# Thirty-two bytes of padding in one tile: moving the right side of SBUF onto multiples of 64 bytes

## The chip, the core and the metric

The kernel runs on one core of a Trainium2 chip. The metric is the device time of one launch in microseconds. A profiled execution of the same program gives its span (from the first to the last instruction) and, for every instruction, the time it took.

## What is computed

One layer of a hybrid backbone over 1024 latent tokens and 256 context tokens with 1024 channels. After an RMS norm with a modulation, one projection of 10272 columns feeds two branches. Branch A is a bidirectional gated delta rule in chunks with a short convolution on q, k and v; branch B is a differential softmax attention of 8 heads with a rotary position code. Each branch is normed, gated with SiLU and projected; the two are merged by sigmoid gates, projected once more and added to the input.

```python
h = rms_norm(x) * (1.0 + scale[:, None]) + shift[:, None]
qkv_a, z_a, a_raw, b_raw, q_b, k_b, v_b, z_b, gates = split_cols(h @ w_in)
o_a, o_ac = gdn_bidirectional(gdn_prepare(...ctx...), gdn_prepare(...latent...), update_ctx)
...
p = jax.nn.softmax(s, axis=-1)
attn = p[:, :, 0] - lam * p[:, :, 1]
return jnp.einsum('bhqk,bkhv->bqhv', attn.astype(v.dtype), v)
...
merged = g_a * (y_a.reshape(b, length, GDN_WIDTH) @ w_oa) + g_b * (y_b.reshape(b, length, DIFF_V_WIDTH) @ w_ob)
return merged @ w_out
```

## The kernel before

**Rounded products.** Nearly all large products are made of three: an operand x is split into a rounded part (type float32r, "xh") and the rest ("xl"), and x·y is taken as xh·yh + xh·yl + xl·yh, added up in PSUM. These are the *rounded products* of the title. Small products of the delta rule and all transposes stay plain float32.

**Streams.** The kernel is written as generators that hand out one instruction at a time with an estimated duration and the tokens it waits for; a planner (`flow`, `turn_flow`) picks the next one by its own model of the engines and so fixes the order on each engine. The estimates are constants in the code; no address enters them.

**Stages in order of time.**

- To about 420 us: loading, the norm, the first projections with the convolution (`mm<-hs,wh`, `mm<-wh,hs`).
- About 420 to 740 us: the projections q, k, v of the attention (`part_flow`, 256 columns wide), beside the preparation of the delta rule (`gdn_prep`).
- About 740 to 1340 us: the gate projections (`fill_flow`, 512 columns wide), beside the scan of the delta rule (`scan`, `out_chunk`).
- About 1340 to 1767 us: the attention and, in between, the merge of branch A. `scores` (L1536) makes `s<-kk,qh` and `s<-kk,ql`: per block of 128 queries and each of the two maps, pieces of 512, 512 and 256 columns. `turns` transposes the weights of the softmax (`t<-ct,S`). `att_out` (L1647) makes `v<-ah,vh`, `v<-al,vh`, `v<-ah,vl`, 256 columns wide, ten key blocks of three products for a pair of query blocks. `merge_` (L1791) makes `ma<-y,wh` and `ma<-y,wl`, 512 wide, 24 products for one bank.
- 1767 to 1856 us: `b_main` (L1909) projects branch B: `mb<-yh,wh`, `mb<-yl,wh`, `mb<-yh,wl`, 512 wide, 384 products.
- To the end: `o_main` (L2097) makes the last projection in seven products of half-size blocks (`x<-...`, `z<-...`, 512 wide).

In a name such as `mb<-yh,wh` the first operand is the one that is streamed through the array and the second is the weights that are loaded ahead of it.

**Where tiles lie.** SBUF is used from two sides. Pools of `side="left"` are stacked upwards from the constants, pools of `side="right"` downwards from a fixed top (`spool`, L711). On the right, from the delta rule on (`gdn_first`, L1047), there stand from the top down: g2 with the tags X, kq and qk (X lowest, qk at the top), g3 and g1, g4 (the scan), later a2 and a0 (the attention: qh, ql, kk, vh, vl and the scores S), and at the end yq (yh, yl), bp and rp. Tags of g2 are used again under other names: X and kq hold kk and qh of every second head, and weights at the end. On the left stand hs and the weights wh, wl of the projections, later a1 (ah, al), yp2 (y), ws2 (wh, wl of the merge and of `b_main`) and lp (half of the operands of `o_main`; the other half is in bp and rp).

The operands' first bytes, as the program places them, modulo 64:

| product | streamed operand | weights |
|---|---|---|
| mm (all projections) | left, 0 | left, 0 |
| s | kk: right, 32 | qh, ql: right, 32 |
| v | ah, al: left, 0 | vh, vl: right, 32 |
| ma | y: left, 0 | wh, wl: left, 0 |
| mb | yh, yl: right, 32 | wh, wl: left, 0 |
| x, z | bh, bl: by turns left, 0, and right, 32 | ah, al: on the same side as bh |

For example kq begins at byte 215008 of each partition, X at 204768, qk at 224224, yq at 121120; ws2 begins at 22528.

Of the kernel before, what the change touches and what calls it, by code (L numbers as in the profile page):

```python
# [17 lines left out]
P = 128  # L18
D = 1024
KT = D // P  # L20
L = 1024
LC = 256
LT = L + LC
# [20 lines left out]
class Block:  # L44
# [1040 lines left out]
    def gdn_prep(self, h):  # L1085
# [6 lines left out]

        def keys():
            S = lambda nm, shape: self.gh[0].tile(shape, F32, tag=nm, name=nm)
            kq, qk = S("kq", [P, LT + L]), S("qk", [P, 2, 2, 2, P])
            kT, qT = kq[:, :LT], kq[:, LT:]
            tk = yield DMA, 3.3, self.kT_t, lambda: nc.sync.dma_start(kq, self.gkq[h])
            tk = tq = self.later(tk, 1.5)
            return kT, qT, qk, tk, tq
        mine = None  # L1100
        if self.gram == h:
            mine = yield from keys()

        te = [None] * 2
        for d in range(2):
# [3 lines left out]
            te[d] = yield ACT, 1.18, [t], lambda: nc.scalar.activation(X[:, d], X[:, d], AF.Exp, scale=-1.0), AF.Exp  # L1109
        yield lambda: self.gram == h  # L1110
        kT, qT, qk, tk, tq = mine or (yield from keys())

        tX, tQ = [[], []], []
# [1097 lines left out]
```

## Time and profile before

| | us |
|---|---|
| median of 3 runs | 1938.72 |
| lowest and highest | 1936.44, 1939.59 |
| the profiled execution's own time | 1938.76 |
| its span | 1936.6 |
| chain from the first mb product to the end of the last x product | 166.0 |

How it is read: the page sums each engine's busy time and follows one chain of waits back from the last instruction. A matmul's recorded duration is longer than the distance to the next one, because the products overlap in the array; the view of one tile lists the least, median and longest duration of a group, and the chain gives start, length and count of a row of products, so that length by count is the distance from start to start. The granted TensorE clock was 1.0 in every stretch of this execution.

### The profile page before, as it was taken

Reading aid. Unit: us, or ns where it says so; the run is one execution under the profiler, and the core shown is the slowest. Engines: PE = TensorE matmul, PEld = TensorE weight load, DVE = VectorE, ACT = ScalarE, POOL = GpSimd, SP = SyncE. Lnnn points to the kernel's source line nnn. Section 1 sums busy time; section 2 is a strip of 40 time slices with the busy share of each in tenths; the row PEclk is TensorE's granted clock in tenths of the full one; section 3 lists DMA queues with packets and bytes.
Section 4 is the critical chain, followed back from the end, with each engine's and each line's share of the span. In section 5 each row is a group of like instructions: output and inputs, shape, how many; then the busy total and the mean of one; then the engine's idle time right before and its main releaser. Section 6 shows DMA issues by size and latency. Waiting matters only on the chain.

```text
span 1936.6 us, 37454 instructions
## 1 busy us (share of the span) xinstructions
PE 1899.9 (98%) x13807; PEld 1673.9 (86%) x13807; DVE 1450.8 (75%) x3613; ACT 1064.0 (55%) x2189; POOL 679.4 (35%) x610
## 2 busy tenths in 40 slices
PE   6999999999999999999999999999999999999999
PEld 4888888899999998888888888888988888888887
DVE  4687998957887887767865865338996979985577
ACT  4543444426233563677576655448885868883222
POOL 3200000005441342343433232326766657671203
PEclk9999999999999999999999999999999999999999
DMA  9144545575545567667785565666336474226542
GB/s 334 56 139 96 138 95 136 125 190 175 168 144 177 183 191 226 226 198 228 213 291 179 192 196 158 214 232 229 127 124 201 165 240 147 83 88 223 184 147 87
DMA packets 383038, 336.39 MB, mean 174 GB/s; under 512 B 142609, under 2 KB 323443, under 8 KB 381831
## 3 DMA queue, kind: packets, MB, share of 16 engines
q1 hardware_dynamic: 382855, 333.99, 55.0%
q8 instruction: 109, 1.79, 0.4%
q14 instruction: 74, 0.61, 0.1%
HBM read 222.14 MB, written 111.79 MB: 172 GB/s over the span
## 4 chain that ended last, share of the span: by engine, by line
PE 84%; DVE 6%; DMA 4%; ACT 3%; issue 2%; POOL 1%; SPq 1%; DVEq 0%; ACTq 0%; POOLq 0%
PE mm L56 42%; PE s L56 7%; PE v L56 5%; PE chain L56 5%; PE mb L56 5%; PE ma L56 4%; PE x L56 3%; PE t L63 3%; PE out L56 3%; PE gram L56 1%; DVE S L1567 1%; DVE ac L595 1%; DMA sk<-gkq 1%; PE pz L56 1%; PE tr L63 1%
## 5 line engine op out<-in xcount | busy, mean ns | idle before, releaser
L56 PE MATMUL mm<-hs,wh 128*128 128x512 f32 (+1 forms) x2048 | 648.3, 390 | 1.5 <-DVE hs L408 1.4
L56 PEld LDWEIGHTS mm<-hs,wh 128*128 128x128 f32 x2048 | 371.1, 189 | 58.6 <-DVE hs L408 2.0
L56 PE MATMUL mm<-hs,wl 128*128 128x512 f32 (+1 forms) x1024 | 397.4, 388 | 1.0 <-POOL wl L886 1.0
L56 PE MATMUL mm<-wh,hs 128*128 128x256 f32 (+1 forms) x1792 | 332.8, 286 | 0.2 <-ACT sq L978 0.2
L56 PEld LDWEIGHTS mm<-wh,hs 128*128 128x128 f32 x1792 | 280.8, 191 | 0.8 <-ACT sq L978 0.5
L1567 DVE TENSOR_SCALAR_CACHE_REDUCE S<-s,rsq 128x512 f32<-128x512 f32 (+1 forms) x384 | 239.5, 654 | 27.6 <-PE s L56 24.9
L56 PE MATMUL mm<-wl,hs 128*128 128x256 f32 (+1 forms) x896 | 255.6, 285 | 0.0
L1604 POOL TENSOR_TENSOR S<-S 128x1280 f32<-128x1280 f32 x64 | 188.9, 2955 | 92.2 <-ACT S L1597 90.9
L56 PEld LDWEIGHTS mm<-hs,wl 128*128 128x128 f32 x1024 | 193.8, 189 | 29.8 <-POOL wl L886 1.4
L1580 ACT ACTIVATE S<-S,mn 128x1280 f32<-128x1280 f32 x128 | 175.2, 1371 | 51.8 <-DVE mn L1579 51.4
L56 PEld LDWEIGHTS mm<-wl,hs 128*128 128x128 f32 x896 | 171.3, 191 | 0.1
L595 DVE SCALAR_TENSOR_TENSOR ac<-xc,convT,ac 128x1284 f32<-128x1284 f32 (+1 forms) x96 | 138.7, 1448 | 11.4 <-ACT ac L593 10.8
L56 PE MATMUL s<-kk,qh 128*128 128x512 f32 (+1 forms) x384 | 142.7, 372 | 1.9 <-DVE S L1567 1.6
L56 PE MATMUL s<-kk,ql 128*128 128x512 f32 (+1 forms) x384 | 133.2, 359 | 0.2 <-DMA ql<-qd 0.2
L1641 DVE TENSOR_TENSOR al<-t,ah 128x512 fp32r<-128x512 f32 (+1 forms) x192 | 106.8, 594 | 7.6 <-ACT ah L1636 6.3
L580 POOL MEMSET xc<- 128x2 f32 (+1 forms) x64 | 3.6, 101 | 298.2 <-ACT sq L629 113.7
L1160 DVE TENSOR_TENSOR ts<-ts,tmp 80x31 f32<-80x31 f32 (+15 forms) x248 | 94.3, 380 | 6.0
L56 PE MATMUL ma<-y,wh 128*128 128x512 f32 x256 | 93.0, 409 | 1.7 <-DVE g L1814 1.7
L1158 DVE TENSOR_TENSOR tmp<-ab,ts 80x31 f32<-80x31 f32 (+15 forms) x248 | 89.2, 360 | 6.8 <-DMA ab<-da 1.4
L1323 ACT ACTIVATE vd<-chain,edk 128x128 f32<-128x128 f32 x144 | 52.3, 370 | 76.1 <-PE chain L56 70.6
L1636 ACT CAST ah<-t 128x512 fp32r<-128x512 f32 (+1 forms) x192 | 88.0, 521 | 8.9 <-PE t L63 8.2
L56 PE MATMUL v<-al,vh 128*128 128x256 f32 x320 | 90.5, 283 | 0.7 <-DVE al L1641 0.6
(296 smaller groups left out, 4312.6 us busy)
## 6 DMA issues: line engine op xcount, KB each, us to landing
wr<-in_w_in_dram SPq DMA_DIRECT2D x48, 512.0 KB, 5.8
hx<-in_w_in_dram SPq DMA_DIRECT2D x64, 256.0 KB, 4.4
x<-xq SPq DMA_DIRECT2D x64, 256.0 KB, 5.2
X<-gcd SPq DMA_DIRECT2D x8, 1280.0 KB, 8.3
kd<-col SPq DMA_DIRECT2D x40, 256.0 KB, 2.2
xq<-X SPq DMA_DIRECT2D x16, 640.0 KB, 8.8
kk<-kd SPq DMA_DIRECT2D x16, 640.0 KB, 6.1
kq<-gkq SPq DMA_DIRECT2D x8, 1152.0 KB
```

The source lines that it names most:

```text
L56: self.nc.tensor.matmul(out, lhsT, rhs, start=start, stop=stop)
L63: self.nc.tensor.transpose(out, src, self.ident[:src.shape[0], :src.shape[0]])
L580: x["e"].append((yield PL1, 0.1, [old], lambda: nc.gpsimd.memset(xc[:, a:b], 0.0)))
L595: t = yield DV2, 1.21e-3 * wd, [t], lambda: nc.vector.scalar_tensor_tensor(ac[:, :wd], xc[:, j:j + wd], self.convw(j, x["ct"]), ac[:, :wd] ...
L1158: t = yield DV2, n * w / 960.0 + 0.08, [t if j else self.later(t, 2.5), t1], lambda: V.tensor_tensor(tv, ab[:, j + 1:, j:j + 1].to_broadca ...
L1160: t = yield DV2, n * w / 960.0 + 0.08, [t, t1], lambda: V.tensor_tensor(ts[:, j + 1:, :w], ts[:, j + 1:, :w], tv, ALU.subtract)
L1323: td = yield ACT, 0.251, [t], lambda: nc.scalar.activation(vd, pc[:, 1], AF.Copy, scale=self.edk[:, c, g:g + 1])
L1567: e = yield DVE, 0.675 if m == 512 else 0.408, [e, self.sfree[c].get(n - 4 + c)], lambda: self.nc.vector.tensor_scalar(x["S"][c][:, o:o + ...
L1580: x["x"].append((yield ACT, 1.36, [e], lambda: nc.scalar.activation(S, S, AF.Exp, bias=x["mn"][:, c:c + 1], scale=-1.0, accum_out=w["l0"][ ...
L1604: e = yield POOL, 2.9, [e], lambda: self.nc.gpsimd.tensor_tensor(S0, S0, S1, ALU.add)
L1636: e = yield ACT, 0.48 if nb == 4 else 0.27, [t, y["old", k]], lambda: self.nc.scalar.copy(y["ah", k][:, :, q], pv)
L1641: t = yield DVE, 0.603 if k < 2 else 0.322, [e, y["old", k]], lambda: self.nc.vector.tensor_tensor(y["al", k][:, :, q], pv, y["ah", k][:, ...
```

## The change

The tile kq of `keys` (in `gdn_prep`) is allocated with eight more float32 values per partition and used without them. It is the first time that kq is allocated, so the slot of the tag in pool g2 grows from 9216 to 9248 bytes.

```diff
         def keys():
             S = lambda nm, shape: self.gh[0].tile(shape, F32, tag=nm, name=nm)
-            kq, qk = S("kq", [P, LT + L]), S("qk", [P, 2, 2, 2, P])
+            kq, qk = S("kq", [P, LT + L + 8])[:, :LT + L], S("qk", [P, 2, 2, 2, P])
             kT, qT = kq[:, :LT], kq[:, LT:]
             tk = yield DMA, 3.3, self.kT_t, lambda: nc.sync.dma_start(kq, self.gkq[h])
```

The top of the right side and qk stay where they are; kq, X and all pools opened below g2 begin 32 bytes lower, at addresses that are multiples of 64 (kq at 214976, X at 204736, yq at 121088). The left side and the right side of the earlier stages (to the end of the convolution) are not moved.

## The prediction

> **What bounds the kernel now.** I read the page first, for which engine is full; then the waits of TensorE, for what is left to gain by supplying it better; then the chain of waits at the end, where the time of one product can be read off.
>
> ```profile
> span 1936.6 us, 37454 instructions
> PE 1899.9 (98%) x13807; PEld 1673.9 (86%) x13807; DVE 1450.8 (75%) x3613; ACT 1064.0 (55%) x2189; POOL 679.4 (35%) x610
> PE 84%; DVE 6%; DMA 4%; ACT 3%; issue 2%; POOL 1%; SPq 1%; DVEq 0%; ACTq 0%; POOLq 0%
> ```
>
> TensorE is busy for 1899.9 of 1936.6 us and is 84% of the chain.
>
> ```profile
> PE mp L56 <- DMA wa<-in_w_ada_dram: 10.6, 1, 10.6
> PE tp L63 <- ACT sil L330: 5.3, 1, 5.3
> PE ma L56 <- DVE g L1814: 1.7, 2, 0.9
> ```
>
> Of its waits the two that count, 10.6 and 5.3 us, are at the very start, before the shifted memory is in use; the next is 1.7 us in all. So behind the front no supplier is late, and the change can act in one way only: through the time that a product itself takes. A product's recorded duration overlaps its neighbours', so I take its time as the distance from start to start, which the chain gives as a piece's length by its count:
>
> ```profile
> 1761.01 5.73 PE ma L56 x24
> 1766.74 89.60 PE mb L56 x384
> 1856.34 21.84 PE x L56 x96
> 1878.18 10.91 PE z L56 x48
> 1889.09 43.66 PE x L56 x192
> ```
>
> From 1766.74 on the chain is TensorE alone, with no idle time. All of these are rounded products of one shape, 128x128 by 128x512. Yet mb takes 89.60/384 = 233.3 ns, and x and z together 76.41/336 = 227.4 ns. The views of the single tiles say the same in durations (least, median, longest):
>
> ```profile
> L56 PE MATMUL mb<-yh,wh x128: 393/396/399, 1766.6 to 1855.5; 128*128 128x512 f32 x128
> L56 PE MATMUL x<-bh,ah x96: 389/389/402, 1856.2 to 1931.9; 128*128 128x512 f32 x96
> L56 PE MATMUL ma<-y,wh x256: 387/395/500, 1350.4 to 1766.1; 128*128 128x512 f32 x128
> L56 PE MATMUL mm<-wh,hs x1516: 277/283/387, 419.7 to 735.6; 128*128 128x256 f32 x190
> L56 PE MATMUL v<-al,vh x320: 276/280/386, 1331.8 to 1755.0; 128*128 128x256 f32 x160
> ```
>
> Not one mb product of 128 is under 393 ns, while the x have their median at 389. What differs is where the operands lie. mb streams yh and yl from the right side, which begin 32 bytes past a multiple of 64, against weights on the left, which begin on a multiple. In x and z both operands lie on the same side: both 32 past, or both on a multiple, at the same 389. So, as these rows have it, it isn't the 32 bytes that cost 6 ns, but that the two operands stand at **different** offsets. The timeline of TensorE shows how the quick pace comes about (columns: start, duration, form, count):
>
> ```profile
> 1856.18 0.40 PE L56 MATMUL x<-bh,ah 128*128 128x512 f32 x1
> ...
> 1858.03 0.39 PE L56 MATMUL x<-bh,al 128*128 128x512 f32 x1
> ...
> 1877.56 0.39 PE L56 MATMUL x<-bl,ah 128*128 128x512 f32 x1
> ```
>
> The first eight products after mb take 1.85/8 = 231.3 ns, the next 86 take 19.53/86 = 227.1 ns. With equal offsets the stream needs some eight products to fall into step; with unequal ones it never does, in 384.
>
> **The change part by part.** It adds 32 bytes to the slot of kq. The right side is stacked downwards from a fixed top, so X in the same pool, and every pool opened below (g1, g3, g4, a0, a2, yq, bp, rp), begins 32 bytes lower, on a multiple of 64; qk, above kq, stays, and no rounded product reads it. No instruction, wait, transfer or queue entry is added or moved, and the planner that orders the streams knows no addresses. What is left is the offsets: mb goes from 32/0 to 0/0, v (left al, ah against right vh, vl) from 0/32 to 0/0; s, x and z keep equal ones; the projections mm and the merge ma lie on the left and don't change.
>
> *mb.* 384 products go from 233.3 to 227.1 ns: 384 x 6.2 = **-2.4 us**. They lie alone on the path:
>
> ```profile
> 1767.00:1856.30 89.30, 89.30 (x384) 71.72 (x384) 48.14 (x58) 18.47 (x27) 18.05 (x10) 1.00 0.58 191
> 1856.30:1936.60 80.30, 76.44 (x337) 62.76 (x335) 65.69 (x72) 22.18 (x24) 18.92 (x12) 1.00 0.31 107
> ```
>
> (Stretch and its length, then busy time of PE, weight loads, DVE, ACT and POOL, granted clock, DMA share, GB/s.) The suppliers of mb are busy for 48.1 of 89.3 us at most, so they can follow a pace 3% quicker; if they couldn't, the gain would be 0. Behind it x starts at once, and its later operands have 10.9 us of x products before them.
>
> *x and z.* They fall out of step at each change of side (mb to x, then between x on the left, x on the right and z); at eight products by 4.2 ns, 34 ns each, four or five such changes are **-0.15 us**, at least 0.
>
> *Attention (1340 to 1767).* Here v, s, ma and the transposes t take turns. The chain gives what 256 columns cost in step and out of it:
>
> ```profile
> 503.19 6.70 PE mm L56 x56
> 509.89 0.44 PE tr L63 x4
> 510.33 4.18 PE mm L56 x35
> 514.51 0.44 PE gram L56 x4
> ```
>
> ```profile
> 1742.65 1.42 PE v L56 x12
> ...
> 1744.29 2.13 PE v L56 x18
> ```
>
> mm, at equal offsets, takes 6.70/56 = 119.6 ns; v, at unequal ones, 2.13/18 = 118.3 ns. At this width being in step is the **slower** pace, by 1.3 ns. So the change costs something in v:
>
> ```profile
> L56 PE MATMUL v<-ah,vh 128*128 128x256 f32 x320 | 90.2, 282 | 0.0
> L56 PE MATMUL s<-kk,qh 128*128 128x256 f32 x128 | 36.6, 286 | 0.3 <-DVE S L1567 0.2
> L56 PE MATMUL s<-kk,qh 128*128 128x512 f32 x256 | 106.2, 415 | 1.6 <-DVE S L1567 1.4
> L56 PE MATMUL ma<-y,wl 128*128 128x512 f32 x128 | 52.3, 409 | 0.0
> ```
>
> v has 3 x 320 products and s 2 x 128 of 256 columns, 1216 in all: +1.6 us if all fall into step. Against them stand 512 of s and 384 of ma with 512 columns: ma's median is 395 where x has 389, because a v, an s or a transpose soon interrupts it; up to 896 x 6 = -5.4 us if none did any more. Between these ends I take what the runs allow: after the change v, s and ma no longer disturb each other, transposes and the small sums still do. v comes in runs of 12 and 18, s and ma in twos to fives: three quarters of the 256-wide (+1.2 us) and a third of the 512-wide at 5 ns (-1.5 us), **-0.3 us**.
>
> *Plain (unrounded) products and transposes.* gram, both operands 32 past, takes 0.44/4 = 110 ns, and tr, both on a multiple, the same 110: **0**.
>
> *The other engines and the DMAs.* They meet the same shift, and rows for both sides stand beside each other:
>
> ```profile
> L1881 DVE TENSOR_TENSOR yl<-yl,yh 128x1024 fp32r<-128x1024 f32 x7 | 8.4, 1215 | 1.7 <-ACT yh L1880 1.7
> L317 DVE TENSOR_TENSOR wl<-wr,wh 128x1024 fp32r<-128x1024 f32 x4 | 4.8, 1215 | 0.0
> ```
>
> ```profile
> g<-gt SPq DMA_DIRECT2D x32, 256.0 KB, 4.1
> x<-in_x_dram SPq DMA_DIRECT2D x16, 256.0 KB, 4.1
> ```
>
> Right (yl, and x of the last stage) and left (wl, g): 1215 ns both, 4.1 us both. **0**.
>
> The sum is -2.4 - 0.15 - 0.3 = -2.85 us. The profiled execution took 1938.76 us (its span 1936.6 and 2.2 around it), as good as the median of the runs, 1938.72: **1936.0 us** after rounding.
>
> **The rivals.** *Addresses don't matter*, and mb is slow for a reason of its own; or the shift doesn't arrive where it should. Then the time is 1938.7. For it: mb and x also differ in what runs beside them, and two groups of products are all that the rows compare. Against it: the pace breaks between one product and the next where ma ends and mb begins, and DVE is busier beside x (65.7 of 80.3 us) than beside mb. The Trainium skill speaks for this rival: its page TensorE: Matmul & The Clock Gate, section Step-by-step: what each phase is for, gives TensorE two independent read ports, so that "Loading the next tile's weights doesn't steal SBUF read bandwidth from the running matmul". By that rule the offset of the one against the other could cost nothing and the sum would be 0; the 393 against 389 ns of these rows don't agree with it, as long as nothing else sets mb apart.
>
> *Step is kept all through attention*, interruptions or not: -2.55 for the end, and two thirds to all of 5.4 us instead of a third, with little of the 1.2 us: 1938.7 - 2.55 - 4.2 = 1932.0. For it: s, v and ma then all have one offset. Against: ma has both operands on multiples of 64 now and still has its median at 395.
>
> *The 256-wide products pay more than mb gains* (slower). The price is 1216 products at the difference of the medians, 283 - 280 = 3 ns, instead of 1.3: +3.6 us against -2.55, 1939.8. It decides from 2.55/1216 = 2.1 ns per product on, if the 512-wide stay out of step. For it: v is on TensorE's path all through attention, with no wait to absorb it. Against: the runs of v and mm in the chain differ by 1.3 ns.
>
> **How the numbers follow.** Forecast 0.60, no effect 0.15 (1938.7), step kept throughout 0.17 (1932.0), 256-wide dearer 0.08 (1939.8). The range runs from 1932.0 to 1940.0: the lower end is the second rival with the upper bound of attention nearly used up, the upper end takes in the other two with the spread of the runs before (1936.4 to 1939.6). About 0.2% of this time, 3.9 us, is what a measurement tells from no change. Faster than that, below 1934.8: most of the second rival and a little of the forecast, 0.20. Slower, above 1942.6: only a corner of the third, 0.02. Within: 0.78.
>
> **What the changed profile would show.** The mb piece of the chain at some 87.2 us for 384, its durations at 389 like x; the piece of x behind it without its slow first eight; v's median going from 280 or 281 to 283; s and ma nearer to 389 in their longer runs; gram, the vector operations and the landings as before. mb still at 396 refutes the whole, v below 280 or ma at 389 throughout would make it faster than I say, and any new wait of TensorE behind the front would mean that the shift made tiles overlap that did not before.

## The result, and the profile after

| | median, us | lowest to highest | runs | against the kernel before |
|---|---|---|---|---|
| before | 1937.53 | 1936.36 to 1942.46 | 22 | |
| after | 1935.56 | 1932.76 to 1938.02 | 22 | 0.9985, 95% interval 0.998 to 0.9991 |

The change makes the kernel faster: by the ratio about 2.9 us (1.7 to 3.9 by the interval), by the two medians 2.0 us. The forecast was 2.7 us below the median of three runs then shown. The profiled execution took 1935.46 us, against 1938.76 before. All runs here and below had a granted clock of 0.998 to 1.0 but two of the twelve of the kernel timed as `e11_timed`, 2075 and 3121 us at 0.853 and 0.56, which its ratio leaves out. On every engine the instructions stand in the same order as before. First the page's span and the chain of waits of the changed kernel, from the first `mb` on:

```profile
span 1933.3 us, 37454 instructions
```

```profile
1766.26 87.04 PE mb L56 x384
1853.30 21.76 PE x L56 x96
1875.06 10.88 PE z L56 x48
1885.94 43.53 PE x L56 x192
```

`mb` takes 87.04/384 = 226.7 ns where it took 233.3: 2.56 us less. `x` and `z` together take 76.17 instead of 76.41 us, also 226.7 ns, and the first piece of `x` no longer has a slow start. The tile views of the same kernel:

```profile
L56 PE MATMUL mb<-yh,wh x128: 389/389/390, 1766.1 to 1852.5; 128*128 128x512 f32 x128
L56 PE MATMUL x<-bh,ah x96: 389/389/390, 1853.1 to 1928.6; 128*128 128x512 f32 x96
L56 PE MATMUL ma<-y,wh x256: 387/396/501, 1349.8 to 1765.6; 128*128 128x512 f32 x128
L56 PE MATMUL v<-al,vh x320: 274/283/388, 1331.2 to 1754.5; 128*128 128x256 f32 x160
```

Every `mb` now stands at 389 or 390 ns. `v` has gone from 280 to 283, and `ma` has not come nearer to 389. To see the rest I took every matmul's distance to the start of the next one and summed by stage (a stage's first product can be taken one earlier or later, which moves both columns of a row alike, by some 0.2 us):

| stage | before, us | after, us | difference |
|---|---|---|---|
| to 420 | 414.8 | 414.8 | 0.0 |
| 420 to 740 | 319.9 | 319.0 | -0.9 |
| 740 to 1340 | 600.3 | 600.7 | +0.4 |
| attention, to 1766 | 426.5 | 426.6 | +0.1 |
| `mb` | 89.6 | 87.0 | -2.6 |
| end | 75.9 | 75.7 | -0.2 |

The stages before the attention hold no rounded product whose operands the change moved. Their differences are chance: in those kernels below that leave the operands of this stage's rounded products as far apart as they were, the stage from 740 to 1340 alone came out between 3.0 us under and 2.5 us over the changed kernel's. The table carries two results: `mb`, and that the attention gained nothing. The piece of `mb` is far steadier than the times of whole runs: it is 87.04 us in all ten profiles of this text in which the addresses of its two operands differ by a multiple of 256 bytes (why this number, the second experiment shows), and 89.0 to 89.6 us in the four others.

### The profile page after: what moved, and what is told of

Read it like the earlier page. It is cut to its first block, busy times and chain, and to the rows that moved or that the text cites. A ratio compares the mean times of both kernels' runs of the same rounds, so it can differ in the third digit from the quotient of the medians.

```text
span 1933.3 us, 37454 instructions
## 1 busy us (share of the span) xinstructions
PE 1896.7 (98%) x13807; PEld 1675.3 (87%) x13807; DVE 1453.0 (75%) x3613; ACT 1062.6 (55%) x2189; POOL 678.8 (35%) x610
## 4 chain that ended last, share of the span: by engine, by line
PE 84%; DVE 6%; DMA 4%; ACT 3%; issue 2%; SPq 1%; POOL 1%; DVEq 0%; ACTq 0%; POOLq 0%
PE mm L56 43%; PE s L56 7%; PE v L56 5%; PE chain L56 5%; PE mb L56 5%; PE ma L56 4%; PE x L56 3%; PE t L63 3%; PE out L56 3%; PE gram L56 1%; DVE S L1567 1%; DVE ac L595 1%; PE pz L56 1%; PE tr L63 1%; SPq L265 1%
```

## The experiments

The theory of the prediction: 512-wide rounded products run 6 to 7 ns faster when their two operands have the same place modulo 64 bytes, and the 256-wide ones some 1.3 ns slower. The rival: the address of one operand, or something else that sets `mb` apart, decides. Below, the *difference* of a product is the address of the streamed operand less that of the weights, modulo 256, whichever side is higher.

### Is it the two operands together?

Two kernels. The first is the changed kernel with `yh` and `yl` alone moved 32 bytes down again:

```diff
         ys = [[self.yq.tile([P, L], F32R, tag=f"{n}{h}", name=n) for n in ("yh", "yl")] for h in range(H)]
+        self.yq.tile([P, 8], F32, tag="pad", name="pad")
```

> The changed kernel with 32 unused bytes at the top of yq: yh and yl of the branch B projection lie 32 bytes past a multiple of 64 again, their weights on one, and everything else stays as in the changed kernel. Theory (a stream of rounded products falls into step only if both operands have the same offset modulo 64): the mb piece of 384 goes from 87.0 back to 89.6 us, the durations of mb from 389 to 393-397 ns, x and z lose their first eight products again (+0.05), and the time is that of before less 0.1 to 0.3 us, some 1938 where the changed kernel has 1935.6. Rival (the gain of 2 us comes from the rest of the shift, attention and the delta rule among it, and mb only happens to be quicker): the time stays at 1935.6.

The second is the kernel *before* with the left side moved by 32 bytes too, so that the attention and the end have equal places but none of their operands begins on a multiple of 64:

```diff
             self.ws, self.yr, side = self.spool(self.ctx, "ws2", 2), self.spool(self.ctx, "yr2", 2), ExitStack()
+            self.ws.tile([P, 8], F32, tag="pad", name="pad", bufs=1)
```

> The kernel before (right side 32 bytes past a multiple of 64) with 32 unused bytes at the start of ws2 on the left, so that from the attention on both sides lie 32 bytes past a multiple: s, v, ma, mb, x and z all have 32/32, and not one operand of theirs is on a multiple of 64. Theory (only the difference counts): mb 87.0 us for 384 at 389 ns, v at a median of 283 ns, time as the changed kernel, some 1935.6 or 0.9990 of before. Rival (a start on a multiple of 64 is what counts, as the change's words have it): mb at 89.6 us or more, ma and x slower too, time at or above that of before.

Measured: 1938.07 us, ratio 1.0002 (0.9993 to 1.0011) for the first, 1936.3 us, 0.9987 (0.9977 to 0.9998) for the second. Their chains at the end, the first kernel's and then the second's:

```profile
1765.47 89.60 PE mb L56 x384
1855.07 21.79 PE x L56 x96
```

```profile
1767.02 87.04 PE mb L56 x384
1854.06 21.76 PE x L56 x96
```

With `yh` 32 bytes away from its place the whole gain is gone, and `mb` is back at the 89.60 us of before to the last digit. With everything on 32 the gain is all there. So beginning on a multiple of 64 bytes is not what helps; the two operands' relation is. The rival "addresses don't matter" falls with the first of the two.

### How equal is equal?

In the third kernel the weights of `mb` and `ma` lie 64 bytes further on in their slots (even blocks) or 16 bytes (odd ones):

```diff
+    def wpair(self, i):
+        o = (16, 4)[i % 2]
+        return [self.ws.tile([P, KT * P + 16], F32R, tag=n, name=n)[:, o:o + KT * P].rearrange("p (k n) -> p k n", k=KT)
+                for n in ("wh", "wl")]
...
-            hi, lo = (self.ws.tile([P, KT, P], F32R, tag=n, name=n) for n in ("wh", "wl"))
+            hi, lo = self.wpair(m)
```

> The changed kernel with the weights of the merge and of the branch B projection moved inside their slots: even blocks of output rows 64 bytes on (0 modulo 64, 64 modulo 128), odd ones 16 bytes on. Theory (modulo 64): mb's 48 products of an even block at 226 to 228 ns from start to start once they are in step, those of an odd block at 233, some 1.2 us more than the changed kernel over mb. Rival (modulo 128): both at 233, 2.5 us more. Rival (16 bytes, the least step at which rows are read): both in step, 87.0 us.

Measured, in one profiled execution, 1940.88 us; `mb` in the chain and in the view of `yh`:

```profile
1769.69 89.04 PE mb L56 x384
```

```profile
L56 PE MATMUL mb<-yh,wh x128: 387/393/398, 1769.5 to 1857.9; 128*128 128x512 f32 x128
```

The even blocks, equal modulo 64, are as slow as the odd ones (231.7 and 232.1 ns from start to start). So the theory as it stood is wrong too: equal modulo 64 is not enough. But the wider slots also made `wh` and `wl` differ from each other, so the difference changed from product to product (64 and 192, 48 and 176). A cleaner kernel keeps the slots and moves the weights' whole pool, and what lies above it on the left, by 128 bytes:

```diff
+            self.ws.tile([P, 32], F32, tag="pad", name="pad", bufs=1)
             st = ExitStack()
```

> The changed kernel with a pad of 128 bytes first in the pool of wh and wl, so that mb's operands differ by 128 bytes (and a multiple of 256), constantly through all 384 products, and v's too; ma, x and z keep a multiple of 256. Theory 64 (the place within 64 bytes counts): mb stays at 226.7 ns, its piece of the chain at 87.0 us. Theory 256: mb is out of step at 232 to 233.5 ns, its piece 89.0 to 89.7 us, and v's mean falls from 118.8 to about 118.2 ns.

Measured, in one profiled execution, 1937.71 us; the chain:

```profile
1765.89 89.59 PE mb L56 x384
1855.48 21.79 PE x L56 x96
```

At a constant 128 bytes `mb` is fully out of step, 233.3 ns. (`v`, 128 bytes apart too, takes 118.5 ns instead of 118.8, where 118.2 was expected.) In the changed kernel the differences of `mb` modulo 2048 are 256, 768, 1280 and 1792 and those of `x` and `z` 0, 512, 1024 and 1536, all in step. So the condition on a product's own two operands is a difference that is a **multiple of 256 bytes**; all others tried at this width, 32, 128 and 224 bytes past one and the mixed row of 48 to 192, were out of step. The change met that condition by luck of what else lies on the two sides: it moved `mb` from 32 to 0 modulo 256, not only modulo 64.

### The other width, and a version that uses it

If 256-wide products are quicker out of step, 2448 of those in the projections can be set apart on purpose. The first try moved their weights 32 bytes up within their slots, all slots being 64 bytes wider:

```diff
-                yield from self.weight(raw, *(self.wab[i % 2].tile([P, KT, W], F32R, tag=n, name=n) for n in ("wh", "wl")),
+                yield from self.weight(raw, *(self.apart(self.wab[i % 2], n) for n in ("wh", "wl")),
...
+    def apart(self, pool, n, far=True):
+        o = 8 if far else 0
+        return pool.tile([P, KT * W + 16], F32R, tag=n, name=n)[:, o:o + KT * W].rearrange("p (k n) -> p k n", k=KT)
```

> The changed kernel with the 256-wide weights of the projections q, k, v of the attention (streamed operand wh, wl) 32 bytes into their slots, hs at 0 as ever: 2448 products of 256 columns at offsets 32/0 instead of 0/0. The theory, turned round: at 256 columns being in step is the slower pace, so out of step they go from 119.8 to about 118 ns, median duration from 283 to 280 or 281, and the time falls by 3 to 4.6 us against the changed kernel, to 1931 to 1932.6, 0.997 of before. Rival (the quicker pace of v in the attention came from its interruptions and not from its offsets): no change, 1935.6. Rival (unequal offsets cost at every width): 1938 to 1945.

Measured: 1938.92 us, ratio 1.0004 (0.9995 to 1.0013). The expected gain did not come, and the gain of the change was gone as well. The next kernel rests on the 256-byte rule: the wider slots had moved weights of the **512-wide** products too. By the addresses in the program, 1216 of these 2688 products had come to a difference of 128 or 192 bytes, and the rest had kept a multiple of 256. It sets the 256-wide ones apart as before but lays out the slots so that every 512-wide product is back at a multiple of 256:

```diff
+    def apart(self, pool, n, far=True):
+        wb = pool is self.wbp
+        o = (0 if far else 56) if wb else 8 if far else 0
+        return pool.tile([P, KT * W + (56 if wb else 64 if n == "wh" else 8)], F32R, tag=n, name=n)[
+            :, o:o + KT * W].rearrange("p (k n) -> p k n", k=KT)
```

> The 256-wide projection products have their weights 32 bytes from hs's place, as in the run before, but the slots are laid so that the weights of every 512-wide product differ from hs by a multiple of 256 bytes again (there they differed by 64, 128 or 192). Theory 256 (products fall into step only where the two operands' addresses differ by a multiple of 256 bytes): the 256-wide products keep the about 118 ns that they had there and the 512-wide ones are back at 226 to 227 ns, so that the 420-740 stage is about 2.6 us shorter than in the changed kernel, the others about 0 to 0.6 shorter; in all 3 to 3.5 us less, about 1932.3 us, 0.997 of the kernel before. Theory 64 (only the place within a block of 64 bytes counts): the 512-wide products were not slowed by their place there but by something else that the layout did, and nothing speaks for its going away: about 1938.5 us.

Measured: 1931.09 us in 5 runs, ratio 0.9968 (0.9955 to 0.998). The same stretches of the chain show both kernels' effect; first the changed kernel, then the first try, then this one. `x92` and `x66` are 512-wide, `x95` is 256-wide:

```profile
714.99 11.39 PE mm L56 x95
...
968.86 14.99 PE mm L56 x66
...
1151.48 21.09 PE mm L56 x92
```

```profile
716.77 11.14 PE mm L56 x95
...
971.21 15.26 PE mm L56 x66
...
1154.49 21.45 PE mm L56 x92
```

```profile
714.49 11.09 PE mm L56 x95
...
967.21 14.99 PE mm L56 x66
...
1150.15 21.09 PE mm L56 x92
```

The 95 products go from 119.9 to 117.3 and 116.7 ns: apart is quicker at this width in both. The 92 products go from 229.2 to 233.2 ns and back to 229.2. Over all products that follow one another, the moved 256-wide ones take 117.8 ns in the first try and 117.1 in the second, instead of 119.8, and the 512-wide ones 231.6 in the first try and 228.1 in the second. By the distances summed over the stages to 1340 us, the first try won 3.2 us on the 256-wide products and lost 7.0 us on the 512-wide ones.

The same version was timed once more, and once with `v` set apart as well (`a1` begins 32 bytes later, `yp2` is padded so that `y` stays at 0):

```diff
             self.yp = self.spool(st, "yp2")
+            self.yp.tile([P, 56], F32, tag="pad", name="pad")
...
         self.a1 = self.spool(st, "a1")
+        self.a1.tile([P, 8], F32, tag="pad", name="pad")
```

> The version with the 256-wide products apart and the 512-wide ones kept, a second time, since its interval (0.9955 to 0.998) touches that of the changed kernel (0.998 to 0.9991, and 0.9969 to 0.9988 beside the run before this). If its gain is the 2400 products at 117 instead of 120 ns, some 3 us or less of them hidden, the ratio is again 0.996 to 0.9975; if it was chance, 0.998 or more.

> As the run above, and the 256-wide products v of the attention too with their operands 32 bytes apart, while y stays a multiple of 256 bytes from its weights. If what keeps the 256-wide ones out of step is worth its 0.6 ns in each of 960 products, 0.4 to 0.6 us less than the run above, about 1931.8 us; if v's neighbours lose what v wins, the same as the run above.

Measured: 1933.8 us, 0.9975 (0.9966 to 0.9984) for the repeat; 1932.32 us, 0.9971 (0.9961 to 0.998) with `v`. All three beat the kernel before, by 5 to 7 us. Against the changed kernel (1935.56 us here, 1936.21 in the last run below) the medians are 1.8 to 5.1 us lower, but the intervals touch or overlap, so that a gain over it of 2 to 3 us is likely and not proven by the times alone. In the repeat's profile the 256-wide products are at 117.1 ns again. With `v` apart the attention is 0.7 us shorter and the total is not.

The stage from 420 to 740 us, forecast to be 2.6 us shorter than in the changed kernel, was only 0.9, 0.0 and 0.2 us shorter in these three profiles. But in each of them a stretch of 3.4 us in that stage (from 599 us on in the first) had a granted clock of 0.5, and 15 or 16 of the 256-wide products took 213 ns: by estimate 16 x 96 ns = 1.5 us. Less that, the stage took 316.6 to 317.6 us, against 318.2 to 320.6 us in the ten profiles that leave these products in step (one of them, the last of the changed kernel, has such a stretch too and is taken less it). So some 2.4 us are gained there. The total of a single profile doesn't show it: the repeat's took 1938.93 us, the longest of its 11 runs, with 2.5 us more than the changed kernel's from 740 to 1340 us.

### Why did the attention gain nothing?

The changed kernel with those two pads alone, so that only `v` is out of step again:

> The changed kernel with v's operands alone 32 bytes apart. If the change cost v 0.5 to 0.6 ns in each of 960 products, v's mean over products that follow one another goes from 118.8 back to 118.2 ns, and the attention from 426.6 to about 426.1 us; if the change cost v nothing, it stays at 118.8 ns. mb stays at 87.0 us.

Measured, in one profiled execution, 1934.66 us, the attention 0.8 us shorter. Two runs of `v` in the chain, before, after, and here:

```profile
1380.67 2.25 PE v L56 x19
...
1419.12 2.01 PE v L56 x17
```

```profile
1380.03 2.27 PE v L56 x19
...
1418.48 2.03 PE v L56 x17
```

```profile
1379.94 2.22 PE v L56 x19
...
1418.30 1.99 PE v L56 x17
```

These 36 products take 118.3, 119.4 and 116.9 ns. So the change did cost `v` about 1 ns in its longer runs (0.5 us over all of `v`), and 32 bytes apart is a little quicker than the 224 of before.

The 512-wide products of the attention remain. `s` moved together with both its operands, so the change left its differences as they were: 0 for three quarters of its products, 192 for the rest (those of `ql` in every second head, where `kk` lies in g2). The last layout brings these to 0:

```diff
-            kq, qk = S("kq", [P, LT + L + 8])[:, :LT + L], S("qk", [P, 2, 2, 2, P])
+            kq, qk = S("kq", [P, LT + L + 56])[:, :LT + L], S("qk", [P, 2, 2, 2, P])
...
         self.a2 = self.spool(st, "a2", 2, side="right")
+        self.a2.tile([P, 16], F32, tag="pad", name="pad", bufs=1)
```

> In the changed kernel a quarter of the products s (those of ql in every second head) still has its operands 192 bytes apart (mod 256). Here that head's buffers are moved so that every rounded product of the attention differs by a multiple of 256 bytes. If these s are what keeps the attention out of step, the 512-wide ones come down from 231-232 to 229 ns or less and the attention from 426.6 us to about 425 us. If it is the plain products and transposes between them, or the change of width within a run, nothing comes of it: s and ma stay at 231 to 232 ns, the attention within 0.4 us of 426.6 us. mb at 87.0 us either way.

Measured, in one profiled execution, 1932.65 us. The attention did not shorten (it is 0.2 us longer), `s` stays at 231.8 ns and `ma` at 230.9. So these `s` are not what keeps it out of step. What shortened was the stage from 740 to 1340 us, to 597.7 us, without a reason that I had. The timed runs settle that:

> The run above again, to tell whether its shorter stage from 740 to 1340 us (3.0 us less than in the changed kernel, in a single profile) belongs to the layout. In the profiles so far that stage went between 0.7 us less and 2.6 us more than in the changed kernel, where no cause by addresses was known for it but in one. If it is chance, the stage is back at about 600 us and the time that of the changed kernel, 0.9985 of the kernel before; if it is the layout, the stage is again at 597 us and the time about 1932.6 us, 0.997.

> The changed kernel as it stands, beside the run above on the same chip: 0.9985 of the kernel before, as it was measured first (0.998 to 0.9991), the mb piece of the chain at 87.0 us.

Measured: 1934.05 us, 0.9979 (0.997 to 0.9988), and 1936.21 us, 0.9979 (0.9969 to 0.9988). The stage is back at 601.8 us, and the ratios are the same: it was chance. A single profile of this kernel tells nothing about 3 us in that stage.

## Why the prediction was right, point by point

- **`mb`, forecast -2.4 us: right.** It measured -2.56 us; the pace in step is 226.7 ns rather than the 227.1 taken from the row of `x`. That this is the operands' relation is shown by taking the gain away with one pad and bringing it about with another.
- **`x` and `z`, forecast -0.15 us: right in its mechanism, the count too low.** -0.24 us. The prediction took four or five changes of side; the trace of before has seven (from `mb` to `x`, then one after every 48 products), each with some seven slow products behind it, and 7 x 34 ns is the 0.24 us. After the change there is not one slow product behind any of them. This says more than the rule of 256: before the change each `x` and `z` already had a multiple of 256 between its own two operands. What changed is that the places of its left and its right side no longer lie 32 bytes apart modulo 256. So a row keeps step only if the next product lies in the same place too; in the kernel with 128 bytes the two sides lie 128 apart, and behind most of these changes one product is slow (231 ns). In the kernel with `mb` apart, `x` starts out of step again: 21.79 us for the first 96 instead of 21.76.
- **The attention, forecast -0.3 us: the mechanism half right, the size wrong; +0.1 us.** Two terms stood against each other. The 256-wide term (+1.2) has the right sign; it measured +0.5 us, since `v` in its short runs is in step only in part: behind a plain product or another width the first `v` takes 117 ns in the changed kernel's trace (median), the next few 118 to 119, and those from the seventh on 120. The 512-wide term (-1.5) failed at the step "after the change v, s and ma no longer disturb each other": it measured about -0.3 us, by the means of `s` (232.4 to 232.1 ns) and `ma` (231.4 to 231.2). Nor did it help to bring every rounded product there to a multiple of 256. The prediction itself has the reason next to that step: the stream needs some eight products to fall into step. The chain of the changed kernel shows the 512-wide ones of the attention in runs shorter than that:

```profile
1360.60 0.70 PE s L56 x3
1362.27 0.69 PE ma L56 x3
...
1400.28 1.25 PE ma L56 x5
```

  These are 230 to 250 ns each. The whole trace bears it out: of the 270 rows of 512-wide rounded products in the attention 263 have eight products or fewer, and in the projections, all at a multiple of 256, the second to fourth product of a row takes 233 or 234 ns (median), and only from the tenth on is it 227. In the longest rows of `ma` it is 227 too. That it is the plain products and the change of width that end a row's step was not tried alone.
- **Plain products, other engines and DMAs, forecast 0: right** within what stages vary by chance: `gram` keeps its median duration of 275 ns, `yl` takes 1216 ns instead of 1215, and the transfers of `g` and `x` land in 4.3 and 4.5 us instead of 4.1, which no stage's time shows.
- **The rivals.** "Addresses don't matter" falls with the pad that undoes `mb` alone. The Trainium skill's page TensorE: Matmul & The Clock Gate, section Step-by-step: what each phase is for, has the weight load take no read bandwidth from the running product. By that rule 32 or 128 bytes between the two operands could cost nothing; here they cost 6.6 ns in each of 384 products. "Step is kept all through attention" and "256-wide dearer" both fall with the +0.1 us of that stage.
- **What was wrong though the number was right:** the place "on a multiple of 64", which I took from the change, and "the same offset" modulo 64, which I read from the rows. Before the change all places were 0 or 32 modulo 64, so its long rows could not tell 64 from 256. `s`, which the prediction listed among those that "keep equal ones", had 192 between its operands in a quarter of its products.
- **Where the number owes something to luck:** the sum of -2.85 us was taken from a median of three runs, 1938.72 us; from the 1937.53 us of the 22 runs it would have given 1934.7 instead of 1936.0, against 1935.56 measured. Within the sum, too little for `mb` and the end (0.25 us) stood against too much for the attention (0.4 us).

## What to carry to other kernels

Where long rows of rounded products run back to back, look at the *difference* of the two operands' addresses and not at either address: with 512 columns make it a multiple of 256 bytes, for each product and from one product to the next, with 256 columns make it not one (32 bytes was the best of those tried), and look after every later change of a slot's size that it stayed so. Expect some 3% on an undisturbed row of at least some ten products and next to nothing on a row that plain products interrupt. A padding that helps one width can cost the other more, so read each width's pace by itself.

## What the runs showed that I had not expected

- Of the differences tried, only multiples of 256 bytes bring step at 512 columns: 226.7 ns in it, 233.3 out of it at 32, 128 and 224 bytes, and 231.9 in the row where 48, 64, 176 and 192 took turns.
- At 256 columns being in step costs 2.7 ns in the projections (119.8 against 117.1 ns at 32 bytes); for `v` it is 118.8 ns at 0, 118.5 at 128, 118.2 at 224 and 117.2 at 32. Why the same alignment helps one width and hurts the other stays open.
- The first rounded product after a plain one is slow. The timeline of TensorE in the changed kernel (start, duration, form, count):

```profile
1385.42 1.25 PE L63 MATMUL t<-ct,S 128*128 128x128 f32 x10
1386.43 0.48 PE L56 MATMUL s<-kk,qh 128*128 128x512 f32 x1
1386.75 0.40 PE L56 MATMUL s<-kk,ql 128*128 128x512 f32 x1
1386.98 0.40 PE L56 MATMUL s<-kk,qh 128*128 128x512 f32 x1
```

From start to start the first `s` takes 0.32 us, the next 0.23. In the whole trace 517 such first products of 512 columns have a median of 316 ns and 65 of 256 columns 202 ns; against 227 and 120 that is 517 x 0.089 + 65 x 0.082 = 51 us by estimate, some twenty times what the change was worth in `mb`. Whether fewer switches between plain and rounded products would bring it in was not tried.
